# A fused decoder step: the query and gate projections as Strassen products over pairs of weight tiles, with keys and values fetched per head from DRAM

## The chip, the cores and the metric

The kernel runs on one core of one Trainium2 chip. The metric is the device time of one execution in microseconds (us). A core has several engines that run side by side and meet only through semaphores: TensorE multiplies matrices (PE in the profile; the loading of its stationary operand is listed as PEld), VectorE (DVE) and ScalarE (ACT) work element by element, GpSimd (POOL) does the same more slowly, and SyncE (SP) issues most of the memory transfers. Each engine works through its own list of instructions in the order in which they were put there. SBUF is the working memory with 128 partitions, PSUM the memory into which TensorE writes its results, and DRAM the large memory outside.

## The reference: what is computed

One inference step of a small decoder with two layers. 512 tokens of a prompt and 8 x 4 sample tokens go through the same weights, so the kernel treats them as 544 columns (T = 544). Layer A is a state-space mixer, and layer B is an attention with three dilations over one shared set of keys and values. The part that the change touches is layer B:

```python
def dilated_mixer(h, attend, biases, g_norm, w_in, w_out):
    u = rmsnorm(h, g_norm) @ w_in                 # 1024 -> 3072 queries + 1024 gates
    q = u[..., :Q_WIDTH].reshape(b, l, 3, KV_HEADS, 128)
    gate = u[..., Q_WIDTH:]
    ...                                           # attention of each dilation group, softmax over groups
    y = o.reshape(b, l, ATT_WIDTH) * jax.nn.silu(gate)
    return y @ w_out
```

`w_in` has 4096 output columns, which the kernel takes as 32 weight tiles of 128: 24 tiles of queries (8 heads x 3 dilation groups) and 8 tiles of gates (one per head). Each tile is multiplied with the normalized activations, 1024 rows (8 chunks of 128) x 544 columns.

## The kernel before

All projections work with split numbers: a 32-bit value is written as a high part in a reduced format and a low part that holds the rest, and a product of two values is made of three passes, high x high, high x low and low x high. Weights are split by `split_w` (L191): ACT casts the high part (L197), DVE subtracts to get the low part (L198). `proj_steps` (L218) issues the three matmuls of each of the 8 chunks. A weight tile is done in two groups of columns, 0 to 256 and 256 to 544 (`HA`, `HB`), so it costs 2 x 8 x 3 = 48 matmuls. The generator stops after each matmul, so that another part of the program can place them one by one.

The work around the change goes like this. After layer A, the loop at L981 makes values (8 tiles, `v_out`), then keys (8 tiles, `k_out`). The value tile lies in a buffer `vt` of a tag with four buffers; the keys are written into two large SBUF buffers `KT`, the transposed values into two more, `Vb`, and the POOL queue regroups the values by position modulo 4 into `Vr` (`regroup`). All these large buffers come from one pool of 13 equal slabs (`half`). Then the loop at L1025 prepares the activations of layer B: for each of 8 chunks DVE scales `h1` into `hb`, a buffer of the same tag as `vt` (L1029), ACT casts the high part `bh` (L1030), and DVE makes the low part `bl` (L1031). These stand after the keys in the program, but the planner may start an instruction earlier when its engine, its inputs and its buffer are free.

In the last stage two streams are woven together. `units` (L1362) are the attention pieces, 49 in all: for each head four blocks of the prompt (`attend`) and two halves of the sample batch (`sample`). `filler` (L1290) is one long stream of matmuls, first the 29 remaining weight tiles (`q_proj`, `gate_proj`), then the output projection `out_proj`. The first three query tiles run ahead of the loop. The loop at L1370 alternates pieces of units with 14 or 15 matmuls of the filler (`FA`, `FB`), with units two ahead (`LA`). The order of the matmuls is held as written; the other engines' orders are chosen by the planner, which gives parts under `high_priority` precedence. `attend` and `sample` read the keys and values from `KT`, `Vb` and `Vr`. The gates of heads are multiplied into the attention result by `gate_mul` and split for the output projection by `y_split`. The sample columns of that input are made in `sample_y`, after the last gate.

Of the kernel before, what the change touches and what calls it, by code (L numbers as in the profile page):

```python
# [20 lines left out]
NB = 8  # L21
# [33 lines left out]
LA, FA, FB = 2, 14, 15  # L55
# [67 lines left out]
def tile_yoco_step(  # L123
# [37 lines left out]
    def f32(ap):  # L161
        return ap.bitcast(F32)
# [118 lines left out]
    vnd = dram.tile([NB, TS, ATH, 128], F32, name="vnd")  # L281

# [661 lines left out]
    KT = [half("kt0"), half("kt1")]  # L944
    Vb = [half("vb0", shape=(128, 4, 4, 128)), half("vb1", shape=(128, 4, 4, 128))]
    Vr = [half("vr0", shape=(128, 4, 4, 128)), half("vr1", shape=(128, 4, 4, 128))]
    vsn = wk.tile([32, ATH, 128], F32, name="vsn", bufs=1)
    def v_out(h, pa, pb):
# [10 lines left out]
        nc.scalar.copy(Vb[h // 4][:, :, h % 4, :], vp)  # L959
        nc.scalar.copy(vsn[:, h, :], vsp[0:32, 0:128])  # L960
        if h % 4 == 3:
            moves.extend((h // 4, r, n) for r in range(4) for n in range(4))

    moves = []

    def regroup():
        for i, r, n in moves[0:3]:
            nc.gpsimd.dma_start(Vr[i][32 * n:32 * n + 32, r], Vb[i][32 * r:32 * r + 32, n])
        del moves[0:3]

    def k_out(h, pa, pb):
        kt = KT[h // 4][:, h % 4, :]
        nc.vector.tensor_tensor(kt[:, 0:HA], pa[:, 0:HA], rs_h[:, 0:HA], op=ALU.mult)
        nc.vector.tensor_tensor(kt[:, HA:T], pb[:, 0:HB], rs_h[:, HA:T], op=ALU.mult)
        dma(kvT[:, h, :], kt)
        yield
# [4 lines left out]
    for i, (f, h, wi) in enumerate(order):  # L981
# [33 lines left out]
        if i > 9:  # L1015
            regroup()
            regroup()
# [4 lines left out]
    b_h, b_l = [half("bh0", F32R)], [half("bl0", F32R)]  # L1022
    b_h.append(half("bh1", F32R))
    b_l.append(half("bl1", F32R))
    for k in range(KD):  # L1025
        tmp = wk.tile([128, T], F32, name="hb", tag="vt", bufs=4)
        hk = h1[k // 4][:, k % 4, :]
        hh, hl = b_h[k // 4][:, k % 4, :], b_l[k // 4][:, k % 4, :]
        nc.vector.scalar_tensor_tensor(tmp, hk, g_b[:, k:k + 1], rs_h, op0=ALU.mult, op1=ALU.mult)  # L1029
        nc.scalar.activation(hh, tmp, AF.Copy)  # L1030
        nc.vector.tensor_tensor(hl, tmp, f32(hh), op=ALU.subtract)  # L1031
# [8 lines left out]
    y_t = [half("y0"), half("y1")]  # L1040
    o_s = half("os", shape=(128, 2, ATH, 128))
    lse = wk.tile([128, 16], F32, name="lse", bufs=1)
# [3 lines left out]
    qpad = [wk.tile([128, NB, 32], F32, name=f"qpad{i}", bufs=1) for i in range(2)]  # L1046
# [4 lines left out]
    qp_t = {}  # L1051
    y_h, y_l = [None, None], [None, None]

    def q_proj(h, g, w):
        if g == 0:
            qp_t[h] = wk.tile([128, 3, SEQ], F32, name="qp", bufs=2)
# [9 lines left out]
    def gate_proj(h, w):  # L1066
        u = y_t[1][:, 3, 0:SEQ] if h == 7 else wk.tile([128, SEQ], F32, name="u", bufs=1)
        for c0, c1 in ((HA, T), (0, HA)):
# [5 lines left out]
            if h == 6:  # L1074
# [3 lines left out]
                if c0:  # L1078
                    sample_y()
# [404 lines left out]
```

## Time and profile before

| | |
|---|---|
| median of 3 runs | 969.93 us (968.3 to 970.86) |
| profiled execution | 973.13 us |
| its span on the core | 971.4 us, 21631 instructions |
| mean granted TensorE clock | 0.988 |
| matmuls | 8833 |
| memory transfers | 159.80 MB, 165 GB/s over the span |

The busy time of an engine is the time in which it had an instruction in work. Matmuls overlap, so the mean length of one (about 290 ns) is not the distance between two; that distance is read from the chain of waits or from the timeline. In rows of groups, the number after the bar is the busy time in us and the mean ns of one, and behind the next bar stands how long the engine sat idle ahead of them and for whom. Line numbers are those of the kernel before.

### The profile page before, as it was taken

How to read it: one execution, taken by the hardware profiler on the slowest of the kernel's cores; microseconds unless marked ns; L12 is line 12 of the kernel's file. 1: busy time of each engine (PE TensorE's matmuls, PEld its weight loads, DVE VectorE, ACT ScalarE, POOL GpSimd, SP SyncE). 2: the span in 40 equal slices, each digit the busy share in tenths (PEclk: the TensorE clock that was granted, in tenths of full speed). 3: DMA queues.
4: the chain of work that ended last, by engine and by line, in shares of the span. 5: the costliest groups of instructions: out<-in, count | busy, mean ns of one | idle time of the engine just before them, and what ended most of it. 6: DMA issues, size and time to landing. Idle time of an engine off the chain costs nothing.

```text
span 971.4 us, 21631 instructions
## 1 busy us (share of the span) xinstructions
PE 944.0 (97%) x8833; PEld 871.5 (90%) x8833; DVE 581.1 (60%) x1194; ACT 443.2 (46%) x939; POOL 234.8 (24%) x334
## 2 busy tenths in 40 slices
PE   7999998999899998999999999999999999999996
PEld 5999887889788888999999999899898898898996
DVE  5688988998899798554544453344344343365422
ACT  5557745754645654322332233443344344445442
POOL 3232545653534632111014300000000000000541
PEclk9999999999999999999999999999999999999998
DMA  7252265254365432545366546667656665663502
GB/s 253 85 135 92 101 204 199 81 179 165 123 197 192 149 134 91 155 142 188 127 213 198 169 134 215 207 202 224 208 190 194 209 218 184 213 203 110 182 30 82
DMA packets 67737, 159.80 MB, mean 165 GB/s; under 512 B 18934, under 2 KB 32584, under 8 KB 67128
## 3 DMA queue, kind: packets, MB, share of 16 engines
q1 hardware_dynamic: 62664, 144.16, 45.6%
q10 hardware_dynamic: 2880, 9.44, 2.5%
q0 software_dynamic: 2096, 4.84, 1.8%
q8 instruction: 69, 1.13, 0.5%
q14 instruction: 28, 0.23, 0.1%
HBM read 134.72 MB, written 21.60 MB: 161 GB/s over the span
## 4 chain that ended last, share of the span: by engine, by line
PE 85%; DVE 7%; ACT 3%; DMA 3%; POOL 1%; issue 1%; DVEq 0%; SPq 0%; ACTq 0%
PE pa L141 32%; PE pb L141 31%; PE sp L141 3%; PE so L141 3%; PE pv L141 2%; PE s L141 2%; PE yd L141 1%; DVE co L524 1%; PE csp L141 1%; PE w L144 1%; PE yo L141 1%; PE ptp L144 1%; PE yos L141 1%; PE xp L144 1%; DVE wlo L198 1%
## 5 line engine op out<-in xcount | busy, mean ns | idle before, releaser
L198 DVE TENSOR_TENSOR wlo<-wraw,whi 128x1024 fp32r<-128x1024 f32 x101 | 126.1, 1248 | 81.6 <-ACT whi L197 78.1
L197 ACT ACTIVATE whi<-wraw 128x1024 fp32r<-128x1024 f32 x104 | 109.9, 1056 | 130.0 <-PE pb L141 89.6
L141 PE MATMUL pa<-xh,whi 128*128 128x256 f32 (+1 forms) x320 | 92.8, 293 | 3.3 <-ACT xh L360 3.3
L141 PE MATMUL pb<-xh,whi 128*128 128x288 f32 (+1 forms) x304 | 91.2, 302 | 3.9 <-ACT cb L326 3.9
L141 PE MATMUL pb<-xl,whi 128*128 128x288 f32 (+1 forms) x304 | 92.0, 304 | 0.9 <-DVE xl L363 0.8
L141 PE MATMUL pa<-xl,whi 128*128 128x256 f32 (+1 forms) x320 | 90.7, 286 | 1.2 <-DVE xl L363 1.2
L141 PE MATMUL pb<-xh,wlo 128*128 128x288 f32 (+1 forms) x304 | 88.3, 303 | 0.0
L141 PE MATMUL pa<-xh,wlo 128*128 128x256 f32 (+1 forms) x320 | 85.0, 283 | 0.0
L141 PE MATMUL pb<-bh,wlo 128*128 128x288 f32 x256 | 77.7, 304 | 0.0
L141 PE MATMUL pb<-bl,whi 128*128 128x288 f32 x256 | 77.6, 303 | 0.0
L141 PE MATMUL pb<-bh,whi 128*128 128x288 f32 x256 | 77.0, 301 | 0.0
L141 PE MATMUL pa<-bl,whi 128*128 128x256 f32 x256 | 74.0, 289 | 0.0
L141 PE MATMUL pa<-bh,wlo 128*128 128x256 f32 x256 | 73.8, 288 | 0.0
L1207 POOL COPY lse<-mxs 128x1 f32<-128x1 f32 x16 | 3.0, 186 | 291.8 <-DVE mxs L1205 291.8
L141 PE MATMUL pa<-bh,whi 128*128 128x256 f32 x256 | 73.5, 287 | 0.0
L141 PEld LDWEIGHTS pa<-xh,whi 128*128 128x128 f32 x320 | 60.8, 190 | 6.3 <-ACT xh L360 3.8
L524 DVE SCALAR_TENSOR_TENSOR co<-cb,cvp,co 128x568 f32<-128x568 f32 x72 | 65.6, 911 | 1.2 <-ACT co L522 0.3
L141 PEld LDWEIGHTS pb<-xl,whi 128*128 128x128 f32 x304 | 58.6, 193 | 6.5 <-issue 4.4
L141 PEld LDWEIGHTS pa<-xl,whi 128*128 128x128 f32 x320 | 60.5, 189 | 3.6 <-DVE xl L363 1.7
L141 PEld LDWEIGHTS pb<-xh,whi 128*128 128x128 f32 x304 | 58.8, 194 | 5.0 <-ACT cb L326 4.1
L141 PEld LDWEIGHTS pb<-xh,wlo 128*128 128x128 f32 x304 | 57.4, 194 | 3.0 <-issue 3.0
L141 PEld LDWEIGHTS pa<-xh,wlo 128*128 128x128 f32 x320 | 58.0, 188 | 1.3 <-issue 0.9
(367 smaller groups left out, 2764.3 us busy)
## 6 DMA issues: line engine op xcount, KB each, us to landing
wraw<-w_in SPq DMA_DIRECT2D x40, 512.0 KB
kc<-ck SPq DMA_DIRECT2D x32, 640.0 KB
vc<-cv SPq DMA_DIRECT2D x32, 640.0 KB
wraw<-wb SPq DMA_DIRECT2D x32, 512.0 KB
s<-s SPq DMA_DIRECT2D x16, 512.0 KB
m<-aed SPq DMA_DIRECT2D x16, 512.0 KB
ssmS<-s ACTq DMA_DIRECT2D x16, 512.0 KB
wraw<-w_out SPq DMA_DIRECT2D x16, 512.0 KB
```

Of the source, the lines that this page charges most:

```text
L141: pin(nc.tensor.matmul(*a, **k))
L144: pin(nc.tensor.transpose(*a))
L197: a = nc.scalar.activation(hi, raw, AF.Copy)
L198: b = lo_eng.tensor_tensor(lo, raw, f32(hi), op=ALU.subtract)
L524: nc.vector.scalar_tensor_tensor(o, cb[:, k:k + n], cvp[:, ti, k:k + 1], o, op0=ALU.mult, op1=ALU.add)
L1207: nc.gpsimd.tensor_copy(lse[:, i16:i16 + 1], mx[:, 2:3])
```

## The change

Strassen's scheme (in Winograd's form) multiplies two matrices, each cut into 2 x 2 blocks, with seven block products in place of eight. Here one matrix is a pair of weight tiles. Its blocks are the first and second four chunks of each of the two tiles. The other matrix is the activation, whose blocks are chunks 0 to 3 and 4 to 7, each in two halves of 272 columns (`TH`). The change has these parts:

- The activations are prepared as seven "quarters", four blocks and three sums of blocks, each 512 rows x 272 columns and each in a high and a low part. For each of four steps: two `hb` buffers, four sums, seven casts, seven low parts.
- A pair of weight tiles gives seven left factors: three of its four blocks as they are, and four sums (`sums`; one of them is written over a block that isn't needed any more). Each is cast and its low part made (`cast`) three products ahead of its use.
- A product is 4 chunks x 3 passes = 12 matmuls of 272 columns. Its result goes into PSUM buffers whose sums, made by ACT and DVE, are the four result blocks. Queries and gates have their own last step (`q_evac`, `gate_evac`).
- 12 pairs of queries and 4 pairs of gates make 16 x 84 matmuls. Two pairs run ahead of the loop, and the loop then takes 12 matmuls of the filler at a time.
- Keys and transposed values are written to DRAM (`kvd`) for each head. `KT`, `Vb`, `Vr` and `regroup` go. `fetch_kv` brings one head's keys, values and regrouped values into one slab with six transfers on SP's queue, three units ahead of that head's first unit; the first two heads are fetched before the loop. The key tile is now a buffer `kt` of the tag of `vt` and `hb`.
- Of the gates only heads 4 and 6 (and 5, 7) are in the last two pairs; the splits of heads whose output buffers don't exist yet are kept in a list (`late_split`) and made when the last pair has given back slabs (`y_alloc`). The first six weight tiles of the output projection go into slabs, the last two into the weight buffers, which was the other way about.

```diff
-LA, FA, FB = 2, 14, 15
+LA, FA, FB = 2, 12, 12
+TH = T // 2
...
     def k_out(h, pa, pb):
-        kt = KT[h // 4][:, h % 4, :]
+        kt = wk.tile([128, T], F32, name="kt", tag="vt", bufs=4)
...
         dma(kvT[:, h, :], kt)
+        dma(kvd[h, :, 0:T], kt)
...
-    for k in range(KD):
-        tmp = wk.tile([128, T], F32, name="hb", tag="vt", bufs=4)
-        hk = h1[k // 4][:, k % 4, :]
-        hh, hl = b_h[k // 4][:, k % 4, :], b_l[k // 4][:, k % 4, :]
-        nc.vector.scalar_tensor_tensor(tmp, hk, g_b[:, k:k + 1], rs_h, op0=ALU.mult, op1=ALU.mult)
-        nc.scalar.activation(hh, tmp, AF.Copy)
-        nc.vector.tensor_tensor(hl, tmp, f32(hh), op=ALU.subtract)
+    quarters = [half(f"bq{j}", F32R) for j in range(7)]
+    def bq(j, k):
+        return quarters[j][:, k, 0:TH], quarters[j][:, k, TH:T]
+    for k in range(4):
+        b1, b2 = (wk.tile([128, T], F32, name="hb", tag="vt", bufs=4) for _ in range(2))
+        for t_, kk in ((b1, k), (b2, k + 4)):
+            nc.vector.scalar_tensor_tensor(t_, h1[kk // 4][:, kk % 4, :], g_b[:, kk:kk + 1], rs_h, op0=ALU.mult, op1=ALU.mult)
+        ts_ = wk.tile([128, 4, TH], F32, name="bt", tag="tb", bufs=2)
+        b11, b12, b21, b22 = b1[:, 0:TH], b1[:, TH:T], b2[:, 0:TH], b2[:, TH:T]
+        s1, s2, s3, s4 = (ts_[:, j, :] for j in range(4))
+        nc.vector.tensor_tensor(s1, b12, b11, op=ALU.subtract)
+        nc.vector.tensor_tensor(s2, b22, s1, op=ALU.subtract)
+        nc.vector.tensor_tensor(s3, b22, b12, op=ALU.subtract)
+        nc.vector.tensor_tensor(s4, s2, b21, op=ALU.subtract)
+        for j, src in enumerate((b11, s2, b21, s3, s1, s4, b22)):
+            hh, hl = bq(j, k)
+            nc.scalar.activation(hh, src, AF.Copy)
+            nc.vector.tensor_tensor(hl, src, f32(hh), op=ALU.subtract)
...
+    def fetch_kv(h):
+        kv_t[h] = kv = half("kv")
+        dma(kv[:, 0, :], kvd[h, :, 0:T])
+        dma(kv[:, 1, 0:SEQ], kvd[h, :, T:T + SEQ])
+        for n in range(4):
+            dma(kv[32 * n:32 * n + 32, 2, 0:SEQ].rearrange("p (r d) -> p r d", r=4),
+                dap(kvd, h * 128 * (T + SEQ) + T + 128 * n, [[T + SEQ, 32], [32 * (T + SEQ), 4], [1, 128]]))
...
+        def sums(p):
+            ro, rp = raws.pop(p)
+            with tc.high_priority():
+                nc.vector.tensor_tensor(s3_, ro[:, 0:4], rp[:, 0:4], op=ALU.subtract)
+                nc.vector.tensor_tensor(rp[:, 0:4], rp[:, 0:4], rp[:, 4:8], op=ALU.add)
+                nc.vector.tensor_tensor(s2_, rp[:, 0:4], ro[:, 0:4], op=ALU.subtract)
+                nc.vector.tensor_tensor(s4_, ro[:, 4:8], s2_, op=ALU.subtract)
+            src[p] = (ro[:, 0:4], s2_, ro[:, 4:8], s3_, rp[:, 0:4], rp[:, 4:8], s4_)
...
+        def product(b, j, o, fresh, last):
+            hi, lo = place(b)
+            for k in range(4):
+                ah, al = bq(j, k)
+                mm(o, hi[:, k, :], ah, start=fresh and k == 0, stop=False, skip_group_check=True)
+                yield
+                mm(o, hi[:, k, :], al, start=False, stop=False, skip_group_check=True)
+                yield
+                mm(o, lo[:, k, :], ah, start=False, stop=k == 3, skip_group_check=True)
+                yield
...
+            for j in range(7):
+                if j == 0:
+                    fetch(p + 1)
+                if j == 4:
+                    sums(p + 1)
+                cast(7 * p + j + 3)
+                key = (0, 1, 0, 2, 3, 4, 3)[j]
+                if key not in ps:
+                    ps[key] = pj("pab"[0:2] if key % 2 == 0 else "pb")[:, 0:TH]
+                o = ps[key]
+                yield from product(7 * p + j, j, o, j not in (2, 6), True)
+                with tc.high_priority():
+                    if j == 0:
+                        nc.scalar.activation(u2, o, AF.Copy, scale=sc)
+                    elif j == 1:
+                        nc.vector.scalar_tensor_tensor(u2, o, sc, u2, op0=ALU.mult, op1=ALU.add)
+                    elif j == 2:
+                        evac(ta, 0, o)
+                    elif j == 3:
+                        nc.vector.scalar_tensor_tensor(u3, o, sc, u2, op0=ALU.mult, op1=ALU.add)
+                    elif j == 4:
+                        evac(tb, 1, o, u3)
+                    elif j == 5:
+                        evac(tb, 0, o, u3, -1.0)
+                    else:
+                        evac(ta, 1, o, u2)
+                if last and j in (0, 2):
+                    y_alloc(j // 2)
+        sample_y()
...
-                wos[m] = load_w(wo[m], None if m < 2 else half("wo", F32R, (128, 2, 8, 128)), nc.gpsimd)
+                wos[m] = load_w(wo[m], half("wo", F32R, (128, 2, 8, 128)) if m < KD - 2 else None, nc.gpsimd)
...
-    for g in range(3):
-        for _ in q_proj(0, g, load_w(wb[g])):
-            pass
     fill = filler()
+    fetch_kv(0)
+    for _ in range(2 * 84):
+        next(fill)
+    fetch_kv(1)
```

188 lines of the change are left out of this document (106 added, 82 removed).

## The prediction

> **What bounds the kernel now.** I read the page's busy shares first, then a table of stretches, then the chain of waits around the two ends of the changed stage. Page, busy time by engine (us, share of the span, instructions):
>
> ```profile
> PE 944.0 (97%) x8833; PEld 871.5 (90%) x8833; DVE 581.1 (60%) x1194; ACT 443.2 (46%) x939; POOL 234.8 (24%) x334
> ```
>
> TensorE never rests over the whole span, but a change in one stage has to be read from that stage. The table of stretches (us, then busy time of PE, weight loads, DVE, ACT, POOL, granted clock, DMA share, GB/s):
>
> ```profile
> 40.00:160.00 120.00, 119.76 (x1082) 111.81 (x1081) 98.36 (x170) 74.41 (x164) 46.45 (x83) 1.00 0.42 132
> 160.00:280.00 120.00, 113.17 (x896) 99.84 (x896) 110.59 (x166) 69.43 (x152) 61.92 (x89) 0.97 0.46 153
> 280.00:390.00 110.00, 107.38 (x874) 96.40 (x874) 93.42 (x148) 57.46 (x114) 50.08 (x49) 0.98 0.44 149
> 480.00:584.00 104.00, 104.00 (x821) 102.84 (x821) 51.37 (x81) 31.20 (x55) 20.83 (x42) 1.00 0.58 185
> 584.00:602.00 18.00, 18.00 (x145) 18.00 (x144) 5.38 (x7) 5.05 (x10) 1.14 (x3) 1.00 0.75 248
> 602.00:660.00 58.00, 58.00 (x716) 51.95 (x715) 22.22 (x86) 25.44 (x62) 0.56 (x3) 1.00 0.61 200
> 660.00:720.00 60.00, 60.00 (x746) 53.43 (x745) 24.08 (x88) 24.04 (x61) 0.60 (x4) 1.00 0.66 202
> 720.00:780.00 60.00, 59.83 (x722) 53.72 (x720) 23.82 (x86) 25.67 (x63) 0.70 (x4) 1.00 0.62 206
> 780.00:840.00 60.00, 60.00 (x744) 53.88 (x743) 23.84 (x89) 25.30 (x63) 0.56 (x3) 1.00 0.64 206
> 840.00:907.00 67.00, 66.06 (x793) 58.70 (x792) 36.74 (x123) 30.69 (x72) 3.16 (x4) 1.00 0.47 154
> ```
>
> The keys-and-values loop is the row 480 to 584; the query and gate projections, with the attention between them, run from 584 to 907. In both, TensorE is busy to within a microsecond and DVE is half idle or more. So fewer matmuls there shorten the run, as long as DVE, which receives the new work, does not become late. The chain of waits across the border between the two loops (start us, us, what):
>
> ```profile
> 578.46 2.83 PE pa L141 x24
> 581.29 3.20 PE pb L141 x24
> 584.49 2.83 PE pa L141 x24
> 587.32 3.20 PE pb L141 x24
> ```
>
> No gap stands at the border: the first query tile starts as the last key tile ends. One weight tile costs 2.83 + 3.20 = 6.03 us for 48 matmuls, 0.118 us each at 256 columns and 0.133 at 288.
>
> **The change part by part.**
>
> *Matmuls.* 32 weight tiles become 16 pairs. A pair now takes 7 products of 4 x 3 matmuls at 272 columns: 84 instead of 96. At the mean of the two cadences, 0.1256 us, a pair takes 10.55 us instead of 12.06; 16 x 1.51 = **-24.1 us**. [...]
>
> *The seven prepared quarters.* Before, the loop at L1025 makes for each of 8 chunks one hb (L1029), one bh on ACT and one bl (L1031). After, each of 4 steps makes two hb of 544 columns, four sums and seven low parts of 272. The nearest rows, these and the ones that later parts use (busy us, mean ns):
>
> ```profile
> L1029 DVE SCALAR_TENSOR_TENSOR hb<-h,gn,rstd 128x544 f32<-128x544 f32 x8 | 6.0, 778 | 0.0
> L973 DVE TENSOR_TENSOR kt<-pa,rstd 128x256 f32<-128x256 f32 x8 | 3.4, 425 | 4.9 <-PE pa L141 4.9
> L974 DVE TENSOR_TENSOR kt<-pb,rstd 128x288 f32<-128x288 f32 x8 | 3.7, 456 | 14.6 <-PE pb L141 14.6
> L1098 DVE TENSOR_TENSOR yl<-y,yh 128x512 fp32r<-128x512 f32 x6 | 4.1, 688 | 2.1 <-ACT yh L1097 2.1
> L1073 DVE SCALAR_TENSOR_TENSOR us<-us,pb 128x32 f32<-128x32 f32 x8 | 1.5, 182 | 1.2 <-ACT us L1072 1.1
> L1098 DVE TENSOR_TENSOR yl<-ys,yh 128x128 fp32r<-128x128 f32 x2 | 0.5, 287 | 0.0
> L1060 ACT ACTIVATE qp<-pa 128x256 f32<-128x256 f32 x24 | 9.2, 383 | 16.0 <-PE pa L141 15.4 <-PE sp L141 0.6
> L1097 ACT ACTIVATE yh<-ys 128x128 fp32r<-128x128 f32 x2 | 0.5, 303 | 0.2 <-DVE ys L1277 0.2
> ```
>
> 272 columns lie midway between 425 and 456: 0.44 us. A step is 2 x 0.78 + 11 x 0.44 = 6.4 us, four are 25.6 us. ACT needs 28 casts, about 0.4 us each, 11 us, and is not the bound. The whole question is **when DVE starts on it**. Product 0 needs quarter 0 of all four steps, so almost all of the preparation. Before, the first four chunks were done well ahead. DVE's timeline shows what released them:
>
> ```profile
> 524.97 0.42 DVE L950 TENSOR_TENSOR vt<-pa,rstd 128x256 f32<-128x256 f32 x1 [1.55 <-PE pa L141]
> 532.24 0.42 DVE L950 TENSOR_TENSOR vt<-pa,rstd 128x256 f32<-128x256 f32 x1 [1.55 <-PE pa L141]
> 532.58 2.17 DVE L1029 SCALAR_TENSOR_TENSOR hb<-h,gn,rstd 128x544 f32<-128x544 f32 x3
> 563.25 0.42 DVE L973 TENSOR_TENSOR kt<-pa,rstd 128x256 f32<-128x256 f32 x1 [0.64 <-PE pa L141]
> 563.59 2.62 DVE L1031 TENSOR_TENSOR bl<-hb,bh 128x544 fp32r<-128x544 f32 x4
> 581.33 0.42 DVE L973 TENSOR_TENSOR kt<-pa,rstd 128x256 f32<-128x256 f32 x1 [0.59 <-PE pa L141]
> 584.70 0.45 DVE L974 TENSOR_TENSOR kt<-pb,rstd 128x288 f32<-128x288 f32 x1
> ```
>
> hb shares its four buffers (tag vt) with the value tiles. Its inputs were there long before, and DVE had idle gaps of 1.55 us in each tile, yet the first hb stands right behind the first write of the last value tile, and three follow at once. In the same way the first bl stands right behind the first write into the second key buffer (kt of head 4), which comes before it in the program on the tag of the slab. I read this as: a buffer of a tag is handed out in program order of the first writes. After the change the key tiles kt also use tag vt, and the last of them, head 7, is first written where the row at 581.33 stands. So the first hb moves from 532.6 to about 581.7, only 3 us before the last key matmul ends, and the cover of the key loop is gone. DVE then has three whole steps, 19.1 us; of the fourth two hb, four sums and the first low part, 3.7; the row at 584.70, 0.45; two low parts of weights with high priority, 1.4; and three weight sums of the second pair, also with high priority, 2.1. That is 26.7 us, to 608.4. Without a wait product 0 would need that last part at about 584.3 + 10 x 0.126 = 585.6. Without the early sums the wait is 20.6, with them 22.7; I take **+21 us**. The ends: 0, if the preparation is done inside the key loop after all, and 27. [...]
>
> *The clock.* A pause of TensorE has a second price. The stretches around the longest pause of the stage before:
>
> ```profile
> 240.00:250.00 10.00, 7.11 (x49) 4.93 (x47) 9.89 (x15) 4.57 (x9) 8.63 (x14) 0.94 0.57 207
> 250.00:260.00 10.00, 10.00 (x73) 8.67 (x72) 7.75 (x12) 7.70 (x17) 5.89 (x9) 0.89 0.29 102
> ```
>
> After 2.9 us idle the clock lost 10 x 0.06 + 10 x 0.11 = 1.7 us. The wait here comes in about four parts, but only short bursts lie between; ends 0 and 3.4, taken **+1.7 us**.
>
> *DVE during the products.* Per query pair: 7 low parts and 4 weight sums of 512 columns at 0.69, 7.6 us; outputs 3 x 0.44 + 2 x (0.41 + 0.18) = 2.5 (before all on ACT). That is 10.1 against two low parts of a whole tile:
>
> ```profile
> L198 DVE TENSOR_TENSOR wlo<-wraw,whi 128x1024 fp32r<-128x1024 f32 x31 | 38.0, 1225 | 31.9 <-ACT whi L197 31.1 <-DMA kc<-ck 0.7
> ```
>
> 2.45 us, so +7.6 for 12 pairs; a gate pair goes from 7.3 (2.45, four outputs of 0.42 and two of 0.18, four products and low parts of 0.69) to 15.2 (7.6, outputs and products 6.0, four split halves of 0.42), +7.9 for 4. In all +123 us on the 136 of the rows from 584 to 907 (less 3 of preparation and a key tile), 256 in 299: 86%. What TensorE loses beside so busy a DVE is bounded by the stage before: with DVE at 82% it idled 0.24 of 120 us, at 92% 6.83 of 120. Ends 0.6 and 17 us for 299. The casts run three products ahead, and the rows from 584 to 907 less 32 x 6.03 leave 130 us of attention for 49 units, 2.7 each, so that one product and the piece behind it take (3.0 + 2.7)/2 = 2.9 us, so I take the lower half: **+5 us**, which also holds the two dense pairs at the start (20 us of DVE in 21 of TensorE).
>
> *The end.* The last product is followed by a chain: gate sum 0.44, tanh 0.38, product 0.41, samples 0.18, product 0.41, sample product 0.42, cast 0.3 and low part 0.29, then the output projection, whose first matmul needs the sample columns. That is 2.8 us, with little beside it on TensorE. The splits of seven earlier heads, 14 halves of 0.42, also wait until the last pair gives slabs back; of their 5.9 us I put some 2.3 into the chain. Before, the same spot had a wait of 1.1 us:
>
> ```profile
> 915.95 0.71 PE L141 MATMUL pv<-vb,pt 128*128 128x128 f32 x4 [1.11 <-ACT pt L1148]
> ```
>
> 2.8 + 2.3 - 1.1: taken **+4 us**; ends 0 (all of it beside other work) and 7.6 (all splits in the chain).
>
> *Keys and values through DRAM.* The 32 POOL transfers vr go, with no one waiting on them. Added on SP's queue: two writes per head in the loop, six reads per head, asked for three units (3 x 5.7 = 17 us) ahead of use. The wait of a fetch is hidden by those units; where such cover failed before, one late load cost
>
> ```profile
> 870.28 5.87 DMA kc<-ck
> ```
>
> 5.9 us. What is queued behind a fetch on SP is the next kc, vc and weights. Ends 0 and 6; taken 0.
>
> **Sum**: -24.1 + 21 + 1.7 + 5 + 4 = +7.6 us. The profiled execution took 973.13 us (span 971.4 and 1.7 around), 3.2 above the median of 969.93; it would become 980.7, and the median **977.5 us**.
>
> **The rivals.** *The preparation is hidden* (ends faster). Place: DVE between 532 and 582. If buffers are not handed out in that order, DVE has 3.9 us free in each 6.03 us key tile, 31 us in eight, enough for 25.6. The first two terms against it shrink to 1, load 4 and end 3 stay: -16, 954 us. For it: DVE is idle enough; against it: both releases shown. It decides from where the wait is under some 13 us, so where the first hb starts before about 573. *Terms nearly cancel*: load and end near their lower ends (0.6 and 1): -24.1 + 20.6 + 1.7 + 0.6 + 1 = -0.2, 970 us. For it: products and attention pieces alternate one to one, and the casts have three products of lead. *DVE bounds the whole stage*: 17 for the load and 7.6 at the end, +23.2, 993 us; for it the row 160 to 280, against it that stage's longer chains. *One late fetch* on top of the forecast: +5.9, 983 us.
>
> **How the numbers follow.** Chances: forecast 0.50 (own range 972 to 985), hidden 0.20, nearly cancelling 0.15, DVE-bound 0.08, late fetch 0.07. A measurement here tells about 0.3%, 2.9 us, from no change. Faster by more: nearly all of hidden, a third of cancelling, a little of the forecast, 0.26. Within: most of the rest of cancelling and a tenth of the forecast, 0.16. Slower: 0.58. The range reaches just past hidden below and almost to DVE-bound above: 952 to 989.
>
> **What would show it.** The first hb behind the last kt, near 582, with TensorE idle some 20 us waiting for a low part of a quarter, and a lower clock digit there; 1344 matmuls on the quarters at about 0.126 us; DVE near 86% between the products; a gap of 3 to 5 us ahead of the output projection. An hb before 560 and no gap at the border would make the prediction wrong; so would waits of product 6 for the output of product 4 all through the stage.

## The result, and the profile after

| | before | after |
|---|---|---|
| median | 969.68 us (968.3 to 970.86) | 1019.11 us (1016.04 to 1020.4) |
| profiled execution | 973.13 us | 1020.4 us |
| its span | 971.4 us | 1018.5 us |
| mean granted TensorE clock | 0.988 | 0.959 |

The changed kernel is slower: the ratio of after to before is 1.0506, with a 95% interval of 1.0478 to 1.0533. The forecast was 977.5 us and its range ended at 989. So the direction was right and the size was not: 49 us for 8.

The span grew by 47.1 us. From first and last matmuls in the timeline it divides like this. The first product starts at 583.28 (first query matmul before: 584.33), -1.0. From there to the last product it takes 365.9 us (949.21) where the projections took 322.8 (907.17): **+43.1**. From the last product to the end of the span it takes 69.3 for 64.2: +5.1. Line numbers from here on are those of the changed kernel, and in the experiments those of their own kernels, a few lines higher where lines were added.

The border first. VectorE's timeline after (start us, us, engine, line, operation, count, idle time before):

```profile
580.28 0.42 DVE L966 TENSOR_TENSOR kt<-pa,rstd 128x256 f32<-128x256 f32 x1 [1.60 <-PE pa L143]
580.62 1.47 DVE L1022 SCALAR_TENSOR_TENSOR hb<-h,gn,rstd 128x544 f32<-128x544 f32 x2
...
583.77 0.45 DVE L967 TENSOR_TENSOR kt<-pb,rstd 128x288 f32<-128x288 f32 x1
```

The first hb stands right behind the first write of the last key tile, as forecast (580.6 for 581.7), and the preparation then fills VectorE. What TensorE waits for there (us in total, times, longest):

```profile
PE pa L143 <- ACT bq L1032: 15.1, 3, 7.7
PE pa L143 <- DVE bq L1033: 3.1, 3, 1.1
```

Now the stages after (busy time of PE, weight loads, DVE, ACT and POOL in each stretch, granted clock, DMA share, GB/s):

```profile
584.00:612.00 28.00, 9.73 (x40) 8.09 (x40) 25.93 (x59) 12.77 (x33) 0.18 (x1) 0.57 0.31 97
612.00:910.00 298.00, 279.87 (x3333) 243.79 (x3335) 206.06 (x638) 137.96 (x321) 4.16 (x20) 0.98 0.66 216
910.00:949.00 39.00, 32.26 (x309) 28.75 (x300) 24.12 (x82) 17.86 (x40) 4.73 (x2) 0.82 0.44 146
```

Before, TensorE rested 1.1 us between 584 and 907 at a clock of 1.00. After, it rests 18.1 + 6.7 = 24.9 us between 612 and 949, and the lower clock takes another 298 x 0.02 + 39 x 0.18 = 13 us, an estimate from the clock digits 0.98 and 0.82 of these two rows. VectorE is busy 206 us in 298, 69%. What TensorE waits for from 612 to 960:

```profile
PE pv L143 <- DVE pt L1261: 10.8, 5, 3.4
PE s L143 <- DMA kc<-ck: 6.5, 6, 2.2
PE so L143 <- DVE wt L1330: 2.9, 3, 1.4
PE pa L143 <- ACT yh L1196: 2.4, 1, 2.4
PE oc L143 <- DVE sbt L1373: 1.8, 1, 1.8
```

Two things carry most of it. pt and wt are attention's transposed weights, copied out of PSUM by short instructions on VectorE. kc are the cached keys of the samples, fetched through SP. In the rows of the weight loads, which start ahead of their matmuls (at 773.95 and 774.07, for example), the waits for kc are larger, 12.2 us between 612 and 910:

```profile
PEld s L143 <- DMA kc<-ck: 12.2, 7, 3.1
```

Why pt is late is seen in VectorE's timeline at one of these waits. The transposes ended near 876.5, and the copy of 0.28 us stands behind six instructions of the products, from 876.98 to 879.84, 2.9 us without a gap:

```profile
876.98 0.69 DVE L1144 TENSOR_TENSOR wlo<-sums,whi 128x512 fp32r<-128x512 f32 x1 [0.36 <-ACT whi L1143]
877.59 0.43 DVE L1103 SCALAR_TENSOR_TENSOR s<-s,pa 128x272 f32<-128x272 f32 x1
877.94 0.68 DVE L1130 TENSOR_TENSOR sums<-wraw,sums 128x512 f32<-128x512 f32 x1
878.54 0.43 DVE L1184 SCALAR_TENSOR_TENSOR sums<-pa,sums 128x272 f32<-128x272 f32 x1
878.89 0.68 DVE L1144 TENSOR_TENSOR wlo<-wraw,whi 128x512 fp32r<-128x512 f32 x1
879.49 0.44 DVE L1110 SCALAR_TENSOR_TENSOR y<-y,s 128x272 f32<-128x272 f32 x1
879.84 0.28 DVE L1261 COPY pt<-ptp 96x128 f32<-96x128 f32 x1
```

Where kc falls behind is seen in SP's own waits between 612 and 910. SP stands at the weight fetch (L190) until a raw buffer (one for a weight tile that isn't split yet) is free, and at vn (the samples' new values, L1295) until the products of the sample before are done; the fetch of kc (L1300) is behind both:

```profile
SPq L190 <- DVE wlo L1144: 43.8, 9, 7.5
SPq L190 <- DVE pt L1261: 24.0, 6, 5.7
SPq L1295 <- PE sp L143: 22.3, 6, 6.6
SPq L1295 <- PE so L143: 19.5, 5, 8.3
SPq L1300 <- PE s L143: 14.8, 3, 9.7
```

The kernel before shows what is new here. From 584 to 907, where kc is L1191, the weight fetch L188 and vn L1186:

```profile
SPq L1191 <- PE s L141: 55.4, 14, 7.2
...
SPq L188 <- DVE wlo L198: 30.2, 8, 7.1
...
SPq L1186 <- PE so L141: 7.4, 1, 7.4
```

Adding up all rows of a line, SP stood 93 us at the weight fetch before and 88 after: that is not new. New are 44 us at vn, for 12, and only 19 us at kc itself, for 56. The time that SP stands at kc, waiting for kc's own buffer, tells how early it gets there. This lead, added up over the fetches, shrank to a third.

### The profile page after: what moved, and what is told of

Same layout as the page of the kernel before. It is cut to its first block, busy times and chain, and to the rows that moved or that the text cites. A ratio compares the mean times of both kernels' runs of the same rounds, so it can differ in the third digit from the quotient of the medians.

```text
span 1018.5 us, 21731 instructions
## 1 busy us (share of the span) xinstructions
PE 946.9 (93%) x8641; PEld 866.0 (85%) x8641; DVE 694.9 (68%) x1490; ACT 470.3 (46%) x993; POOL 216.7 (21%) x303
## 5 line engine op out<-in xcount | busy, mean ns | idle before, releaser
L143 PE MATMUL pa<-bq,whi 128*128 128x272 f32 x512 | 111.4, 310 | 18.3 <-ACT bq L1032 15.1
L199 ACT ACTIVATE whi<-wraw 128x1024 fp32r<-128x1024 f32 x72 | 76.1, 1057 | 106.0 <-PE pb L143 69.3
L200 DVE TENSOR_TENSOR wlo<-wraw,whi 128x1024 fp32r<-128x1024 f32 x69 | 86.9, 1259 | 50.7 <-ACT whi L199 48.1
L143 PEld LDWEIGHTS pa<-bq,whi 128*128 128x128 f32 x512 | 84.6, 197 | 21.5 <-ACT bq L1032 16.0
L143 PE MATMUL pb<-bq,whi 128*128 128x272 f32 x384 | 84.3, 315 | 0.0
L143 PE MATMUL pa<-bq,wlo 128*128 128x272 f32 x256 | 75.9, 296 | 0.0
L143 PEld LDWEIGHTS pb<-bq,whi 128*128 128x128 f32 x384 | 65.4, 203 | 1.4 <-issue 0.4
L1143 ACT ACTIVATE whi<-wraw 128x512 fp32r<-128x512 f32 x64 | 40.2, 628 | 50.6 <-PE pb L143 20.0
```

What stands on the lines that cost most here:

```text
L143: pin(nc.tensor.matmul(*a, **k))
L199: a = nc.scalar.activation(hi, raw, AF.Copy)
L200: b = lo_eng.tensor_tensor(lo, raw, f32(hi), op=ALU.subtract)
L1143: nc.scalar.activation(hi, src[p][j], AF.Copy)
```

## The experiments

The theory has three separate parts: **the border** (the order in which buffers of tag vt are handed out), **VectorE's queue** (attention's copies behind the products' work, which stands ahead by priority) and **SP's queue** (kc behind vn and the weights). The rivals: VectorE's load as such, or the bytes of the reads of keys and values, whatever the order. Each set of runs has its own runs of the kernel before beside it, so ratios to these are compared; that of the change itself is 1.0506.

### The border: kt on another tag

```
-        kt = wk.tile([128, T], F32, name="kt", tag="vt", bufs=4)
+        kt = wk.tile([128, T], F32, name="kt", tag="xk", bufs=2)
```

> The key tiles kt take the two buffers of tag xk, which the value loop uses before, and the tag vt stays with the value tiles and hb. If the border wait comes from the order in which buffers of vt are handed out: the first hb near 532 us instead of 580.6, TensorE's wait of some 21 us for the low parts of the quarters under 2, the half clock behind it (1.8 us) gone, the time 1019.1 - 21.5 - 1.8 = 996, and the stage behind as long as before (product 0 to last product 343 us). If instead VectorE cannot take 25.6 us of preparation beside the key tiles: the first hb early, but a wait of 10 or more left, 1005 to 1010, and key tiles that come late. If the later losses of the stage are a consequence of the border (pairs that run late, a lower clock): more than 23 us gained, 985 or less.

Measured: 994.26 us, ratio 1.0257 (1.0192 to 1.0322), some 24 us less. The first hb moves by 49 us, and at the border TensorE no longer waits for a quarter; the 3.3 us of rest in the stretch below are one wait of the attention. VectorE's timeline, and the stretch at the border:

```profile
531.20 1.47 DVE L1022 SCALAR_TENSOR_TENSOR hb<-h,gn,rstd 128x544 f32<-128x544 f32 x2
```

```profile
584.00:610.00 26.00, 22.67 (x193) 22.07 (x194) 22.00 (x49) 13.07 (x24) 1.39 (x4) 0.99 0.61 191
```

The hand-out order of the tag was the cause, and VectorE takes the whole preparation beside the key tiles. The profiled execution was the longest of the four (1002.5; the others 989.7 to 996.7); from its first product to its last it took 349.4 us, where the change's 365.9 less the 23 of the border leave 343. So the later losses do not go with the border.

### VectorE's queue: copies first, more cover, less load, another place

Attention's copies with high priority:

```
+        with tc.high_priority():
             nc.scalar.copy(pt[:, 0:nk, :], tp[:, 0:nk, :])
             nc.vector.tensor_copy(pt[0:w, 2, :], tp[0:w, 2, :])
...
+        with tc.high_priority():
             nc.scalar.copy(wt[:, 0:4, :], w1)
...
```

> Attention's copies of transposed weights out of PSUM (pt and wt, on VectorE and ScalarE) get the same high priority as the casts, weight sums and outputs of the products; nothing else is changed. If the stage loses because these short copies stand in the queue behind the products' VectorE instructions: TensorE's waits of pv and so for pt and wt on VectorE (15.2 us between 606 and 960) fall under 6, the lost clock falls with them, 1019 becomes 1004 to 1010. If VectorE's load itself is the limit: what the copies gain the products lose (TensorE then waits for weights or for an output buffer), within 3 us of 1019.

Measured: 1008.17 us, ratio 1.0391 (1.0366 to 1.0416), 11 us less, with the same instructions and the same load. The waits for pt are gone from TensorE's list between 612 and 960, and those for kc grew from 6.5:

```profile
PE s L143 <- DMA kc<-ck: 9.5, 9, 2.8
PE so L143 <- DVE wt L1332: 1.4, 2, 0.9
```

More products between the transposes and their use:

```
-LA, FA, FB = 2, 12, 12
+LA, FA, FB = 2, 18, 6
```

> FA, FB = 18, 6 for 12, 12: between the transposes of a unit's weights and the product with the values stand 18 matmuls of the fillers (2.3 us) for 12 (1.5 us); the total per unit stays 24. If pv waits because 1.5 us is too short a cover for copies that stand behind three or four VectorE instructions of 0.4 to 0.7 us: the waits of pv for pt on VectorE (11 to 12 us) fall under 4, the time becomes 1007 to 1012. If the products then run out of weights or output buffers, or the wait moves to the next part of a unit (the scores, op): the sum of TensorE's waits in the stage stays, within 3 us of 1019.

Measured: 1009.13 us, ratio 1.0401 (1.0356 to 1.0445), 10 us less. TensorE's waits from 612 to 960:

```profile
PE s L143 <- DMA kc<-ck: 9.3, 6, 2.9
PE pv L143 <- DVE pt L1261: 4.7, 8, 1.3
```

pv's waits for pt fell by more than half, the transposes now wait for the scores (2.8 and 2.5 us; FB became short), and kc rose. So 1.5 us of cover was too short for the queue it had to hide.

The weight sums on POOL:

```
-                nc.vector.tensor_tensor(s3_, ...
+                nc.gpsimd.tensor_tensor(s3_, ...   (and the three others)
```

> The four weight sums of a pair run on POOL instead of VectorE: 2.8 us less of VectorE per pair, 44 us over the 16 pairs (busy 695 to 651). If VectorE's load is what the stage lost by (pt and wt stand behind sums and low parts): its waits for pt and wt on VectorE fall from 16 to under 8 and the time to 1005 to 1011. If only the order in VectorE's queue counts: as long a wait as before, 1016 to 1022. If POOL's slower sums make weights late: TensorE waits for wlo, over 1022.

Measured: 1010.52 us (1006.37 to 1020.88), ratio 1.046 (1.039 to 1.053). The median lies in the range named for the load, but the interval is too wide to tell 0 from 11 us; in the profiled execution (1006.37) pv's waits for pt were 7.3 us, two long ones. It is no clean test of the load either. 64 instructions of 0.69 us, 44 us, left VectorE, but its busy time fell only from 694.9 to 674.5 us, because others became longer. The same low parts from 612 to 890, in the change and with the sums on POOL:

```profile
L1144 DVE TENSOR_TENSOR wlo<-wraw,whi 128x512 fp32r<-128x512 f32 x54 | 37.2, 688 | 5.8 <-ACT whi L1143 4.3
L1144 DVE TENSOR_TENSOR wlo<-wraw,whi 128x512 fp32r<-128x512 f32 x55 | 46.3, 842 | 9.1 <-ACT whi L1143 6.4 <-DMA bt<-bvd 0.4
```

The first weight sum of a pair pinned behind what stands before it in the program:

```
-                nc.vector.tensor_tensor(s3_, ro[:, 0:4], rp[:, 0:4], op=ALU.subtract)
+                hold(nc.vector.tensor_tensor(s3_, ro[:, 0:4], rp[:, 0:4], op=ALU.subtract))
```

> The first weight sum of the next pair is pinned on VectorE behind what stands before it in the program (the output of product 3), where before it was placed one or two steps earlier, by priority, as soon as the plan took the weight tiles for landed. Nothing is added or removed. If VectorE standing at the sums, and the burst of four sums and casts ahead of attention's copies, is what pv and so wait for: their 16 us fall under 9, the time becomes 1008 to 1013. If the place of the sums does not matter: within 3 us of 1019. If weights then come late: TensorE waits for wlo, 1022 or more.

Measured: 1017.62 us, ratio 1.0499 (1.0444 to 1.0553): no difference from the change. In the profiled execution, the longest of the four, the waits for pt were 14.8 us and those for kc 1.5. The place of the first sum alone is not it; the copies ahead of the whole burst, above, brought 11 us.

### SP's queue: reads left out, another order, another queue

The keys and values of head 0 for all heads, which leaves out 42 of the 48 reads (and so makes another output):

```
     def fetch_kv(h):
+        if h:
+            kv_t[h] = kv_t[0]
+            return
```

> The keys and values of head 0 are used for all heads: 42 of the 48 reads from DRAM are left out, so the output of the heads 1 to 7 is not the reference's; every other instruction stays. If the reads cost what the prediction took (0, ends 0 and 6): 1013 to 1019. If the stage's waits for kc, or for values, come from these reads on SP's queue or on the DMA engines: the waits for kc fall under 2 us and the time under 1012. If the queue order on VectorE is the cause of the rest: pv's waits for pt stay at 11 to 13 us.

Measured: 1007.18 us, ratio 1.0385 (1.0354 to 1.0415), 12 us less. The prediction gave these reads 0, ends 0 and 6.

All reads kept, kc ahead of vn:

```
-        dma(vn, ...)
...
             dma(kc[jp], ck[h, q, :, 2 * jp:2 * jp + 2, :])
+        dma(vn, ...)
```

> The fetch of the cached keys kc is put ahead of that of vn in the program, so that SP no longer stands at vn (one buffer, released by the products of the sample before; 42 us of SP's waits) before it issues kc. If kc is late because of the order on SP: the waits for kc (12.2 us at the weight loads) fall under 4, as with the reads of keys and values left out (3.6), and the time becomes 1006 to 1011 with those reads kept. If the bytes of those reads on the DMA engines are the cause: the waits for kc stay above 8 and the time within 4 us of 1019.

Measured: 1011.11 us, ratio 1.0428 (1.0388 to 1.0468), 8 us less. The weight loads' waits for kc, here first with kc ahead of vn, then with the reads left out, both from 584 to 910, for 12.2 us in the change:

```profile
PEld s L143 <- DMA kc<-ck: 5.0, 4, 1.4
```

```profile
PEld s L143 <- DMA kc<-ck: 3.6, 2, 3.1
```

So the order alone, with every byte still moved, brings most of what the missing reads brought. (SP's lead at kc stays at some 20 us with the new order and is 42 without the reads, so the lead goes with the waits for kc, but not one to one.)

Keys and values through DRAM alone, in the kernel before (same writes and reads as in the change, kt on the tag xk, no Strassen products):

```
-    KT = [half("kt0"), half("kt1")]      (and Vb, Vr, regroup)
...
+        dma(kvd[h, :, 0:T], kt)
...
+    def fetch_kv(h):
...
-            mm(pv, pt[:, i, :], Vb[h // 4][:, b, h % 4, :], ...)
+            mm(pv, pt[:, i, :], vb[:, b, :], ...)
```

> The kernel before with keys and values through DRAM alone (same writes, same six reads per head, three units ahead; kt on the tag xk, so that hb keeps its place; no Strassen products). If that part costs what the prediction took (0, ends 0 and 6): 967 to 973, waits for kc under 3 us. If it costs by itself what leaving the reads out of the changed kernel gave back (12 us): 978 to 984, with waits for kc.

Measured: 973.43 us beside 971.2, ratio 1.0024 (1.0006 to 1.0042), 2.3 us, and 0.6 us of waits for kc at the weight loads. By itself this part costs what the prediction allowed; in the changed kernel, leaving the reads out gave back 12 us. SP's waits show a difference. In this run SP stands 55 us at vn, but only 37 at the weight fetches, and kc keeps a lead of 38 us. With the pairs on top (the change) the weight fetches take 88 us, and the lead is 19.

Two runs moved transfers to POOL's queue. The weights:

```
-                raws[p] = [fetch_w(wb[i]) for i in pairs[p][1]]
+                raws[p] = [fetch_w(wb[i], nc.gpsimd.dma_start) for i in pairs[p][1]]
```

> The raw weight tiles of the pairs are fetched from POOL's queue instead of SP's. SP stood 100 us of the stage at the weight fetch (three raw buffers, two taken per pair), with cache keys kc behind it. If that is why TensorE waits for kc (6.5 us, and 12.2 at the weight loads): these waits fall under 2, SP's waits at the weight fetch disappear, 1019 becomes 1008 to 1012. If kc is late because its two buffers come free late, or because the transfers themselves take long beside the fetches of keys and values: the waits for kc stay within 2 us of 6.5 and the time within 3 us of 1019.

The samples' caches:

```
-        dma(vn, ...)
+        nc.gpsimd.dma_start(vn, ...)      (and so for kc and vc)
```

> The cached keys, cached values and new values of the samples (kc, vc, vn) are fetched from POOL's queue, weights, biases and keys and values of the prompt stay on SP's. If kc is late because it stands on SP behind weight fetches and the six reads of keys and values: the waits for kc (6.5 us at the matmuls, 12.2 at the weight loads) fall under 3, without the harm of the run with the weights on POOL's queue (there VectorE stood 21.8 us at the weight sums, since the weights came late behind POOL's copies of lse): 1019 becomes 1006 to 1011. If the reads of keys and values slow the transfers themselves: waits for kc as before, 1016 to 1022.

Measured: 1030.69 us, ratio 1.0635 (1.0597 to 1.0674), and 1033.49 us, ratio 1.0659 (1.0622 to 1.0697): both slower than the change, although TensorE's waits for kc fell to under 1 and to 2.5 us. VectorE's waits between 612 and 910 say where it went, first with the weights, then with the caches moved, for 2.9 us in the change:

```profile
DVE sums L1127 <- DMA wraw<-wb: 21.8, 10, 5.9
```

```profile
DVE sums L1127 <- DMA wraw<-wb: 19.1, 9, 4.5
```

The planner had put the weight sums on VectorE as early as it took the tiles for landed. They landed later, and VectorE stood, and attention's copies stood behind it: TensorE waited 16.0 and 14.0 us for pt and 6.7 and 7.7 for wt. Why the tiles landed later is less sure: in the first run POOL stood 67.0 us at its copies of lse (the samples' softmax sums), with weight fetches behind them, while for the second run this was not followed.

### Together

kt on xk, copies first, caches on POOL's queue:

> Three edits together: kt on the tag xk (alone 994.3), attention's copies with high priority (alone 1008.2), the samples' caches on POOL's queue. If the losses are separate terms, they add: 1019.1 - 24.8 - 10.9 - (8 to 13) = 970 to 975, and with TensorE's idle time in the stage under 8 us the lost clock goes too, 960 to 970. If they stand in for each other (the second wait ends when the first one is gone): 980 to 990.

Measured: 993.12 us, ratio 1.0255 (1.0206 to 1.0303): slower than either of the two expectations; VectorE still stood 13.9 us at the sums.

kt on xk, copies first, the sums pinned, kc ahead of vn (the four edits above in one kernel):

> Four edits together: kt on the tag xk, attention's copies with high priority, the sums pinned, kc ahead of vn. If border, VectorE's order and SP's order are separate terms: 1019 less 25, 11 and 8 to 12 is 971 to 975, TensorE's waits in the stage under 8 us; less the lost clock that goes with the waits, 960 to 970. If another shared limit stands behind them (DMA bytes, VectorE's load): 980 to 992, with waits of another name in their place.

Measured: 978.54 us (974.18 to 982.2), ratio 1.0082 (1.0054 to 1.0109). Alone the four gave 24, 11, 1 and 8 us by their ratios, 44; together 41 of the 49 us. So they add, as far as the intervals tell (that of the first alone is 6 us to either side).

The same with FA, FB = 16, 8:

> The four edits and FA, FB = 16, 8: 2.0 us of products for 1.5 between a unit's transposes and its product with the values. If what is left of the waits after the four edits is a copy that comes late: 3 to 8 us less than with the four alone. If it is nothing of that kind: within 3 us of it.

Measured: 976.2 us, ratio 1.006 (1.0024 to 1.0096): not told apart from the run without it.

The same as that, with the sums on POOL for pinned on VectorE, and then with the chain of combine under high priority as well (some twenty short instructions that work out the weights of the samples' three dilation groups, for the matmuls oc):

```
     def combine():
+        with tc.high_priority():
             nc.scalar.activation(lsm, lsm, AF.Ln)
...
```

> kt on the tag xk, attention's copies first, kc ahead of vn, FA, FB = 16, 8, and the weight sums on POOL (for pinned on VectorE). If VectorE's load is what is left: TensorE's waits for VectorE and ScalarE fall, the time becomes 962 to 970, below the kernel before. If only the places in VectorE's queue mattered, and these are already right: 974 to 979 as with the sums pinned. If POOL's sums make weights late: 980 or more.

> As the run with the sums on POOL, and combine's chain on VectorE and ScalarE with high priority. If the end of the stage is long because this chain of some twenty short instructions stands behind the gate outputs and splits of the last three pairs: the wait of oc and the half clock behind it (8 to 10 us lost between 888 and 915) shrink, 4 to 8 us less than without. If the half clock comes from the sum of the small waits there, whatever combine does: within 3 us of it.

Measured: 983.88 us, ratio 1.0125 (1.0095 to 1.0154), and 979.15 us, ratio 1.0078 (1.0058 to 1.0097). The first is slower than the run with the sums pinned (1.006). In its profile TensorE rested 4.6 us in 12 behind the first pair, 2.7 of them for kc and 1.9 for qpad, which VectorE writes. That the sums on POOL came late there was not shown:

```profile
600.00:612.00 12.00, 7.38 (x66) 4.98 (x66) 4.99 (x16) 3.50 (x6) 6.44 (x6) 0.76 0.71 237
```

VectorE's busy time fell by 18 us here (687.2 to 669.6), not by 44, so this doesn't settle what its load costs; the last run does. Combine's place brought some 5 us.

Combine first with the sums pinned on VectorE, and that with the pairs' weights on POOL's queue, which the copies of lse leave for ScalarE:

```
-        nc.gpsimd.tensor_copy(lse[:, i16:i16 + 1], mx[:, 2:3])
+        nc.scalar.copy(lse[:, i16:i16 + 1], mx[:, 2:3])
```

> The four edits, FA, FB = 16, 8 and combine's chain with high priority. If combine's place sets the end of the stage: 970 to 973 (976.2 without it). If it does not: 974 to 978.

> The four edits, FA, FB = 16, 8, combine's chain with high priority, and the weight tiles of the pairs fetched from POOL's queue with nothing else on it (the copies of lse go to ScalarE). If what is left of the waits for kc (10.7 us at the weight loads) comes from SP standing at weight fetches: these waits fall under 2 and the time is 6 to 10 below e17, 960 to 968 and so below the kernel before. If the transfers themselves are late (bytes): waits for kc or for weights stay, within 3 us of e17.

Measured: 972.43 us, ratio 1.0018 (1.0004 to 1.0032), and 970.24 us, ratio 1.0009 (0.9993 to 1.0025): 2 us apart and not told apart, where 6 to 10 were expected. The waits for kc fell to 0.4 us at the matmuls and from 10.7 to 1.3 at the weight loads, as expected, but between 600 and 620 TensorE now rested 6.4 us:

```profile
600.00:620.00 20.00, 13.61 (x110) 12.06 (x109) 10.54 (x31) 6.57 (x14) 0.53 (x1) 0.83 0.50 167
```

The weights of the third pair came late there. Its second tile was asked for at 596.1, 3 us later than from SP, when SP, free of the weights, had sent cache fetches at 592.2 to 594.3; VectorE stood 4.3 us for it and took it up at 604.4. Last, the first three pairs from SP and the rest from POOL's queue:

```
-        raw = wpool.tile(...); dma(raw, src)
+        raw = wpool.tile(...); q(raw, src)      (q is nc.gpsimd.dma_start for pairs 3 to 15)
```

> As the run with the weights alone on POOL's queue, but the tiles of the first three pairs come from SP's queue, where no cache key stands behind them yet. If the two stalls (6.4 us at 600 to 620, and the waits for kc of 10.7 us at the weight loads) are independent: 970.2 less 5 to 7, 963 to 966, faster than the kernel before by 0.5%. If the late start only hid other waits: 968 to 972, no difference from the kernel before.

Measured: **959.8 us** (955.58 to 966.64) beside 970.19, ratio 0.9896 (0.9861 to 0.993): faster than the kernel before by 1.0%, with the same Strassen products, sums and reads as the change, and by more than expected (963 to 966). The same tile goes out at 597.0 here, ahead of the cache fetches at 599.2, and VectorE takes it up at 601.3 without a wait. Its page (busy time by engine), its stretches, and the waits of TensorE that are left between 584 and 960:

```profile
PE 924.3 (96%) x8641; PEld 850.0 (89%) x8641; DVE 689.7 (72%) x1490; ACT 472.1 (49%) x1009; POOL 227.4 (24%) x313
```

```profile
584.00:612.00 28.00, 28.00 (x249) 26.84 (x248) 23.40 (x56) 15.45 (x30) 2.50 (x6) 1.00 0.78 260
612.00:860.00 248.00, 246.50 (x3164) 216.38 (x3163) 183.10 (x589) 127.63 (x310) 12.66 (x24) 1.00 0.75 238
860.00:888.00 28.00, 25.83 (x268) 23.19 (x269) 21.30 (x81) 16.76 (x38) 0.58 (x1) 1.00 0.48 165
```

```profile
PE pa L143 <- ACT yh L1196: 6.2, 1, 6.2
PE ptp L146 <- DVE s L1251: 1.4, 3, 0.7
...
PE s L143 <- DMA kc<-ck: 0.4, 1, 0.4
```

VectorE has 1490 instructions here as in the change, and is busier in the stage (183 us in 248, 74%, for 69%), because the stage is shorter. TensorE rests 1.5 + 2.2 = 3.7 us in it, for 24.9, at a clock of 1.00. A VectorE as busy as that does not have to hold TensorE up. SP stands 18 us at the weight fetches here, and kc has its lead again, 63 us. What is left is the gap of 6.2 us ahead of the output projection: from the last product to the end of the span it takes 72.0 us, for 64.2 before.

## Why the prediction was wrong, step by step

**Matmuls, -24.1: held, to within 3 us.** 8641 matmuls for 8833. In the last run, where little else disturbs, the stage from first to last product takes 304.0 us (584.23 to 888.25) for 322.8, 18.8 less, with 2.6 us more rest. That makes 21.4; the other 2.7 us were not traced.

**Preparation at the border, +21, and the clock there, +1.7: held.** Product 0 was done near 606.2 where it would have been near 584.8 without a wait, 21.5 us; the clock of 0.50 lasted to 610.5, some 1.8 us (18 matmuls in 4.08 us from 606.40, where 18 x 0.126 make 2.27). The mechanism (the tag's hand-out order, read from two releases in the trace of before) is shown by the run with kt on another tag. The size of an instruction, taken from rows that read PSUM (425 and 456 ns), held for the sums and low parts between SBUF buffers: 446 to 452 ns. The rival that the preparation is hidden fell for this kernel; a change of one tag makes it true.

**VectorE during the products, +5: this is the step that failed.** The load was somewhat too high: measured are 25.9 + 206.1 + 24.1 = 256 us between 584 and 949, but 21 of them are the preparation at the border, which the forecast's 256 leaves out, so it is 235 for 256. (The forecast adds up lengths, 0.69 us each, while the next instruction often starts after 0.61.) A load that was too high cannot explain a loss that was too low: wrong was how a time was made of it. I bounded the loss by a stage with as high a share of busy time, and took the lower half because "the casts run three products ahead". The casts were not late; no wait for them is in the list. Late were attention's copies, which share VectorE's queue and have less precedence: pt and wt cost TensorE 10.8 + 2.9 us and a little more. Their cover had been cut by the change itself, from FA = 14 matmuls to 12, 1.5 us, while 2.9 us of the products' work stood ahead of one of them. With the copies first, the waits for pt went and 11 us came back, and in the last run 1490 instructions in another order, with more cover, leave 3.7 us of rest. So the price was one of order, and the share of busy time did not give it. The rival that VectorE bounds the whole stage (993 us) named the engine, but fell as a mechanism too: VectorE was 69% busy in the stage that lost and 74% in the fastest run, where TensorE rested 1.5 us in 248.

**Keys and values, 0 (0 to 6): right alone, wrong in company.** Alone they cost 2.3 us (0.6 to 4.1). In the change about 12 came back without the reads, and 8 with kc ahead of vn. There SP stood 88 us at weight fetches and 44 at vn, with kc behind, and kc's lead shrank from 56 us to 19. The prediction named what is queued behind a fetch of keys and values on SP, kc among it, and took 0. It did not ask how much lead kc had and what else on SP would take of it. "One late fetch" at 5.9 us was the right kind of event; it came seven times at up to 3.1.

**The clock, beyond the border: missing.** Some 13 us in the stage. The low digits stand behind pauses that the two points above made, as far as the stretches show; the clearest is 0.50 from 896 to 900, behind the 3.4 us that pv waited for pt up to 895.7. The prediction priced a lower clock for one pause only.

**The end, +4 (0 to 7.6): the size held**, 5.1, but partly by luck. TensorE rests 2.6 us more behind the last product than before (11.9 for 9.3), with a gap of 2.4 us ahead of the output projection where 3 to 5 were named. The granted clock there was 0.89 for 0.96, and for this the prediction had no term.

The account, an estimate from these rows: 24.9 us of rest less 1.1 before, 5.7 us of waits for kc that stand only in the rows of the weight loads (12.2 less 6.5), and 13 us of clock, 42.5 in all, against 44 (43.1 + 24.1 - 21.5 - 1.7) that the stage lost beyond border and matmuls. The clock's share is read from two digits, so that it is good to some 2 us.

Of the signs named beforehand, the late hb and the gap at the border came; VectorE near 86% did not (69%). The range was too narrow because its terms were bounded one by one for work that shares queues.

## What to carry to other kernels

When a change puts work on an engine or a queue that runs in order, ask which short instruction of another stream now stands behind it, and what cover that instruction has, in us (here a copy of 0.28 us stood behind 2.9 us of others, under a cover of 1.5); the busy share does not say it. On a DMA queue, list every fetch that stands for a buffer and what is behind it, and read the lead of a fetch from the time that the queue stands at it, before asking what the new bytes cost (here kc's lead went from 56 us to 19). And a new tile under an old tag can move the first write of a later tile of that tag: here the first hb stood at 580.6 for 531.2, and the one word was worth some 24 us.

## What the runs showed of the hardware that was not expected

**The clock halved behind pauses of 1.8 us and less.** In the changed kernel TensorE's longest pause from 910 to 931 is the one of 1.8 us ahead of oc. Three stretches of it:

```profile
921.00:929.00 8.00, 5.46 (x60) 4.84 (x60) 7.43 (x29) 3.24 (x10) 0.00 (x0) 1.00 0.15 51
929.00:931.00 2.00, 2.00 (x19) 2.00 (x19) 0.62 (x2) 0.92 (x2) 0.00 (x0) 1.00 0.49 118
931.00:941.00 10.00, 10.00 (x60) 9.34 (x58) 2.93 (x11) 2.12 (x4) 2.36 (x1) 0.52 0.63 221
```

After 2.5 us of rest in 8, in pieces (and 1.5 in the 6 before), TensorE is busy without a gap and runs at half the clock for ten us, while it does the oc matmuls of 16 columns between products. In the run with combine first and the sums pinned the pause ahead of oc is gone, TensorE rests 2.0 us in the ten before, and the same oc matmuls ran at full clock:

```profile
880.00:890.00 10.00, 10.00 (x94) 9.51 (x93) 6.94 (x22) 4.52 (x12) 0.00 (x0) 1.00 0.27 68
```

Elsewhere in the changed kernel a clock of 0.50 (896 to 900) stands behind one pause of 3.4 us, that of pv for pt. Here no pause was longer than 1.8, so that shorter ones, added up, may have been enough; that is a guess from these stretches, and whether the narrow matmuls took part was not tried.

**VectorE took 2.35 us for 0.4 us of work beside one POOL instruction.** At the end of the changed kernel (both engines' timelines):

```profile
941.72 2.37 POOL L200 TENSOR_TENSOR wo<-wraw,wo 128x1024 fp32r<-128x1024 f32 x1 [2.09 <-ACT wo L199]
...
941.99 2.35 DVE L1103 SCALAR_TENSOR_TENSOR s<-s 128x240 f32<-128x240 f32 x1 [0.97 <-ACT s L1099]
944.38 0.41 DVE L1110 SCALAR_TENSOR_TENSOR y<-y,s 128x240 f32<-128x240 f32 x1
```

An instruction that takes 0.4 us at this size (the median of its row on L1103 is 407 ns) took 2.35, to just behind the end of POOL's. In the last run a low part of y of the same size took 2.54 us in the same way, and it is a part of the 6.2 us gap that is left there. In the kernel before, a product of 128x256 took 1.91 us from 909.66 on, beside a POOL instruction from 908.90 to 911.29, where the other of that size on its line (L1088) took 0.43. And in the first run with the sums on POOL, VectorE's low parts took 842 ns on average for 688. What couples the two engines in these rows was not shown; a version that keeps such instructions apart was not tried.
